# Reading the moving operand of 48 projection units in a woven token order, and dividing the matmuls of four units at token 192

## The chip, the cores and the metric

The kernel runs on one core of one Trainium2 chip. The metric is the device time of one execution in microseconds, lower being better. Before the change it is 1238.59 us (median of two runs, 1238.34 and 1238.84).

## The reference

One inference step of a one-layer decoder: a Mamba-2 SSD branch and a causal pooling branch, each gated per channel, summed and projected. There are 336 tokens: 16 meta tokens, 256 prompt tokens and 64 sample tokens (8 sequences of 8). After the first stages only the last 320 count. Width is 2048. Cut to what matters here:

```python
proj = xn @ w_in                       # 2048 -> 13344 columns
z_ssd, xbc, dt_raw, z_pool, u, gate_ssd, gate_pool = split(proj)
...                                    # conv, SSD recurrence, gated group norm: y
branch_ssd = y @ w_proj_ssd            # 2048 x 2048
mixed = einsum(pooled(u), pool_mix_w) + pool_mix_b      # four groups of 512 x 512
p_out = mixed * pool_scale * silu(z_pool)
branch_pool = p_out @ w_proj_pool      # 2048 x 2048
merged = sigmoid(gate_ssd) * branch_ssd + sigmoid(gate_pool) * branch_pool
h_new = h + merged @ w_out             # 2048 x 2048, then an RMS norm
```

## The kernel before

Everything is kept transposed: channels on the 128 partitions, tokens along the free axis. The weight matrices are cut into **units**, each of which makes 128 output channels for all tokens from 2048 input channels. A unit is 16 k-tiles of 128 x 128 weights, loaded in two halves of 512 KB. The list `UNITS` (`_units()`) fixes the order by hand: `B`, `C`, `xs` and `z` first, with the SSD stages woven between them, then `gs` (gate of the SSD branch, 16 units) alternating with `br` (`w_proj_ssd`), then `u`, `zp` (the pooling branch's z, 16 units) and `mix`, then `gp` (gate of the pooling branch, 16 units, the last zp and mix among the first of them), then `bp` (`w_proj_pool`, 16 units) and `wo` (`w_out`, 16 units).

Precision is kept by splitting each float32 operand into a rounded part `hi` and a rest `lo`, both of type float32r. For each k-tile `half_k` issues three matmuls into the same PSUM tile `acc`: `hi` weights times the high part of the data (L212), `hi` weights times the low part (L213), `lo` weights times the high part (L214). Their moving operands are `xh`/`xl` for projections of the input, `yh`/`yl` for `br`, `ph`/`pl` for `bp` and `mh`/`ml` for `wo`. A unit is thus 48 matmuls. From `gs` on the moving operand is 128 x 320 in most units, read token after token from SBUF (a projection of the input starts at token 16, `NMETA`).

Weights arrive on SP's DMA queue (`raw`). ScalarE rounds each half to `hi` (L144), and VectorE subtracts to get `lo` (L150), about three halves ahead of their use, from rings of four buffers. `acc` is a ring of three PSUM tiles. A unit is evacuated right after it, while the next one runs: `gs_evac` (L760), `zp_evac` (L736) and `gp_evac` (L773) are one ScalarE activation each, 128 x 320 from PSUM to SBUF, and `bp_evac` (L781) multiplies by the gate on VectorE. The program's order on each engine is the order in which this code issues it (`manual_schedule`); `at`, `later` and `tick` put an evacuation and its followers a quarter of a unit or more behind.

Matmuls outside the units matter for reading the profile: the sum over tokens at the end (L817, a 128 x 128 float32 stationary operand and a moving operand of one column), the sum of squares over channels for the group norm (L672, float32, 320 columns), and some in the SSD stages. A float32 matmul is shown by the trace as two MATMUL rows, a float32r matmul as one.

## Time and profile before

| | before |
|---|---|
| median of the runs | 1238.59 us |
| span of the profiled execution | 1239.1 us |
| PE busy, weight loads busy | 1203.4 us, 1165.4 us |
| DVE, ACT, POOL busy | 728.4, 557.7, 159.4 us |
| MATMUL rows, LDWEIGHTS rows | 8066, 8066 |
| first gs evacuated, last | 413.7 us, 602.8 us |
| first zp evacuated, last | 696.1 us, 879.6 us |
| first gp evacuated, last | 888.0 us, 998.8 us |
| matmuls of bp | 997.9 to 1110.5 us |

Engines: PE is TensorE's matmuls and PEld its weight loads, which have rows of their own; DVE is VectorE, ACT ScalarE, POOL GpSimd, SP the queue of DMA issues. Matmul rows overlap: a row lasts from its first token until its result is written, and the next one starts long before that. So the distance from one start to the next (called pitch below) tells what a matmul costs in a full stream, and the duration of a row does not. The profiled execution's span is 0.5 us above the median of the runs.

### The profile page before, as it was taken

The numbers are of one execution on the slowest core, as the hardware profiler recorded it, in microseconds if no ns is written. First come the engines' busy times: TensorE is split into PE (matmuls) and PEld (weight loads), VectorE is DVE, ScalarE is ACT, GpSimd is POOL, SyncE is SP. The second block draws the span as 40 slices with busy tenths as digits, with TensorE's granted clock in tenths as the row PEclk, the third lists the DMA queues.
The fourth block names the chain that finished last, engine by engine and source line by source line (L and its number), as shares of the span: only waits on it lengthen the run. The fifth ranks groups of instructions, "written<-read, shape, count | busy, mean of one in ns | idle before, by whom it ended". The sixth has DMA issues, their size and how long they took to land.

```text
span 1239.1 us, 19826 instructions
## 1 busy us (share of the span) xinstructions
PE 1203.4 (97%) x8066; PEld 1165.4 (94%) x8066; DVE 728.4 (59%) x1008; ACT 557.7 (45%) x792; POOL 159.4 (13%) x161
## 2 busy tenths in 40 slices
PE   6999999999999999999999999999999999999995
PEld 4988988888988999999999999999999999999995
DVE  8798789888887733433445465564343345554543
ACT  4356575748474633333334443434343333334441
POOL 7251142425344000000000000000000000000000
PEclk9999999999999999999999999999999999999998
DMA  5335637475746444444456545554444444456432
GB/s 221 125 125 182 219 126 257 146 243 170 246 143 212 152 156 151 154 153 144 150 161 174 161 150 164 156 156 153 154 153 150 144 149 154 152 170 208 151 120 85
DMA packets 82715, 202.49 MB, mean 163 GB/s; under 512 B 26512, under 2 KB 31280, under 8 KB 82608
## 3 DMA queue, kind: packets, MB, share of 16 engines
q1 hardware_dynamic: 82256, 199.58, 49.9%
q0 software_dynamic: 368, 1.65, 0.4%
q8 instruction: 63, 1.03, 0.3%
q14 instruction: 28, 0.23, 0.1%
HBM read 186.34 MB, written 15.32 MB: 163 GB/s over the span
## 4 chain that ended last, share of the span: by engine, by line
PE 83%; DVE 7%; issue 5%; POOL 3%; ACT 1%; DMA 1%; DVEq 0%; SPq 0%; POOLq 0%; ACTq 0%
PE acc L212 27%; PE acc L213 26%; PE acc L214 26%; DVE lo L150 2%; POOL hin L624 2%; DVE cacc L320 1%; DVE wl L230 1%; DVE x L282 1%; DMA raw<-wall 1%; PE ps_st L565 1%; PE ps_y L579 1%; POOL ss L667 1%; DVE hn L955 0%; POOL bm L482 0%; DVE hin L632 0%
## 5 line engine op out<-in xcount | busy, mean ns | idle before, releaser
L150 DVE TENSOR_TENSOR lo<-raw,hi 128x1024 fp32r<-128x1024 f32 x312 | 392.6, 1260 | 352.6 <-ACT hi L144 352.5
L144 ACT ACTIVATE hi<-raw 128x1024 fp32r<-128x1024 f32 x312 | 329.8, 1058 | 530.5 <-PE acc L213 438.3
L212 PE MATMUL acc<-xh,hi 128*128 128x320 f32 (+4 forms) x1536 | 480.5, 313 | 0.0
L213 PE MATMUL acc<-xl,hi 128*128 128x320 f32 (+4 forms) x1536 | 477.9, 311 | 0.0
L214 PE MATMUL acc<-xh,lo 128*128 128x320 f32 (+4 forms) x1536 | 476.9, 310 | 0.7 <-DVE lo L150 0.7
L212 PEld LDWEIGHTS acc<-xh,hi 128*128 128x128 f32 x1536 | 288.8, 188 | 2.6 <-issue 1.3
L214 PEld LDWEIGHTS acc<-xh,lo 128*128 128x128 f32 x1536 | 288.9, 188 | 1.0 <-DVE lo L150 1.0
L213 PEld LDWEIGHTS acc<-xl,hi 128*128 128x128 f32 x1536 | 288.7, 188 | 1.2
L213 PE MATMUL acc<-pl,hi 128*128 128x320 f32 x256 | 79.4, 310 | 0.0
L214 PE MATMUL acc<-ph,lo 128*128 128x320 f32 x256 | 79.3, 310 | 0.0
L212 PE MATMUL acc<-mh,hi 128*128 128x320 f32 x256 | 79.2, 309 | 0.0
L213 PE MATMUL acc<-ml,hi 128*128 128x320 f32 x256 | 79.1, 309 | 0.0
L214 PE MATMUL acc<-mh,lo 128*128 128x320 f32 x256 | 79.1, 309 | 0.0
L212 PE MATMUL acc<-ph,hi 128*128 128x320 f32 x256 | 79.1, 309 | 0.0
L212 PE MATMUL acc<-yh,hi 128*128 128x320 f32 x256 | 78.7, 308 | 0.0
L213 PE MATMUL acc<-yl,hi 128*128 128x320 f32 x256 | 78.7, 308 | 0.0
L214 PE MATMUL acc<-yh,lo 128*128 128x320 f32 x256 | 78.7, 308 | 0.0
L624 POOL TENSOR_TENSOR hin<-hin,E 128x512 f32<-128x512 f32 x32 | 50.9, 1618 | 52.4 <-ACT E L542 41.9
L320 DVE SCALAR_TENSOR_TENSOR cacc<-rawf,par,cacc 128x360 f32<-128x360 f32 (+1 forms) x72 | 49.1, 682 | 2.1 <-ACT cacc L316 0.4
L212 PEld LDWEIGHTS acc<-ph,hi 128*128 128x128 f32 x256 | 48.4, 189 | 0.0
L213 PE MATMUL acc<-wl,hi 128*128 128x336 f32 (+1 forms) x128 | 43.7, 341 | 4.8 <-DVE wl L230 4.7
L214 PEld LDWEIGHTS acc<-ph,lo 128*128 128x128 f32 x256 | 48.2, 188 | 0.0
(221 smaller groups left out, 1436.8 us busy)
## 6 DMA issues: line engine op xcount, KB each, us to landing
raw<-wall SPq DMA_DIRECT2D x312, 512.0 KB, 3.5
hin<-ssmT SPq DMA_DIRECT2D x16, 512.0 KB, 6.8
ossms<-hin SPq DMA_DIRECT2D x16, 512.0 KB, 5.8
bc<-acT SPq DMA_DIRECT2D x8, 672.0 KB, 6.9
hn<-xT SPq DMA_DIRECT2D x4, 640.0 KB, 6.9
x<-xT SPq DMA_DIRECT2D x3, 672.0 KB, 8.2
opool<-u SPq DMA_DIRECT2D x16, 100.0 KB, 3.1
oconv<-rawf SPq DMA_DIRECT2D x24, 45.5 KB, 4.0
```

What stands on the lines that cost most here:

```text
L144: S.activation(hi, r, AF.Copy)
L150: V.tensor_tensor(out=lo, in0=r, in1=hi.bitcast(F32), op=ALU.subtract)
L212: PE.matmul(acc[:, :n], lhsT=hi[:, c], rhs=bh, start=first, stop=False)
L213: PE.matmul(acc[:, :n], lhsT=hi[:, c], rhs=bl, start=False, stop=False)
L214: PE.matmul(acc[:, :n], lhsT=lo[:, c], rhs=bh, start=False, stop=last)
L230: V.scalar_tensor_tensor(out=wl[q][:, c, :], in0=xg[q][:, c, :], scalar=pc("norm_w", k), in1=wh[q][:, c, :].bitcast(F32), op0=ALU.mult, op ...
L282: V.scalar_tensor_tensor(out=x, in0=x, scalar=pc("norm_w", k), in1=rstd, op0=ALU.mult, op1=ALU.mult)
L320: V.scalar_tensor_tensor(out=a[:, a0:], in0=r[:, a0 + k:k + ACCW], scalar=pc("conv_w", 4 * c + k), in1=a[:, a0:], op0=ALU.mult, op1=ALU.add)
L565: PE.matmul(p, lhsT=st["bt"][:, i, :], rhs=st["xdt"][:, i, :], start=(i == 0), stop=False)
L579: PE.matmul(p[64 * e:64 * e + 64, a:b], lhsT=st["xdt"][:n, i, 64 * hh:64 * hh + 64], rhs=m[:n, e, o:o + b - a], start=(i == 0), stop=(i == ...
L624: GP.tensor_tensor(out=hv, in0=hv, in1=E, op=ALU.mult)
L667: later(1, lambda: GP.tensor_tensor(out=gn[g], in0=gn[g], in1=sq, op=ALU.add))
```

## The change

`WEAVE` names a run length for three kinds of unit: 2 for `gs`, 4 for `zp`, 16 for `gp`. Their moving operand's 320 tokens are seen as two halves of 160, and each matmul reads a run of that many tokens from the first half, then as many from the second, then the next run of the first, and so on. With runs of two the order is 0, 1, 160, 161, 2, 3, 162, 163 and so on. The read from SBUF thus has three dimensions. The output view has the same shape but its columns lie in a row in PSUM, so the result stands there in woven order, written without a jump. The three evacuations read PSUM in the order that undoes it (`unwoven`) and write the old layout. Each of the three kinds has 16 units, that is 768 matmuls.

For `bp` units 12 to 15, `half_k` issues each of the 48 matmuls twice, over tokens 0 to 191 and 192 to 319, with the same weights. Some comment lines are dropped as well. Nothing else differs, and the weights, loads and evacuations of other units stand where they stood.

```diff
@@ -63,6 +63,7 @@
 UNITS = _units()
+WEAVE = {"gs": 2, "zp": 4, "gp": 16}
...
@@ -206,9 +207,28 @@
-    def half_k(acc, w, kk, bh, bl, n, first, last):
+    def woven(a, r, c):
+        return a.rearrange("p (r j c) -> p j r c", r=r, c=c)
+
+    def unwoven(a, r, c):
+        return a.rearrange("p (j r c) -> p r j c", r=r, c=c)
+
+    def half_k(acc, w, kk, bh, bl, n, first, last, weave=0, cut=False):
         hi, lo = w
         c = slice(128 * kk, 128 * kk + 128)
+        if cut:
+            for h, l, f, e in ((hi, bh, first, False), (hi, bl, False, False), (lo, bh, False, last)):
+                for j in range(2):
+                    t = (slice(0, 192), slice(192, n))[j]
+                    PE.matmul(acc[:, t], lhsT=h[:, c], rhs=l[:, t], start=f and j == 0, stop=e, skip_group_check=True)
+            return
+        if weave:
+            bh, bl = woven(bh, 2, weave), woven(bl, 2, weave)
+            o = acc[:, :n].rearrange("p (j r c) -> p j r c", r=2, c=weave)
+            PE.matmul(o, lhsT=hi[:, c], rhs=bh, start=first, stop=False)
+            PE.matmul(o, lhsT=hi[:, c], rhs=bl, start=False, stop=False)
+            PE.matmul(o, lhsT=lo[:, c], rhs=bh, start=False, stop=last)
+            return
         PE.matmul(acc[:, :n], lhsT=hi[:, c], rhs=bh, start=first, stop=False)
...
@@ zp_evac
-        S.activation(pool["z", g][:, c, :], acc[:, 0:TV], AF.Silu)
+        w = WEAVE["zp"]
+        S.activation(pool["z", g][:, c, :].rearrange("p (r j c) -> p r j c", r=2, c=w), unwoven(acc[:, 0:TV], 2, w), AF.Silu)
@@ gs_evac
-        S.activation(t, acc[:, 0:TV], AF.Sigmoid)
+        w = WEAVE["gs"]
+        S.activation(t.rearrange("p (r j c) -> p r j c", r=2, c=w), unwoven(acc[:, 0:TV], 2, w), AF.Sigmoid)
@@ gp_evac
-        S.activation(gpv[q][:, c, :], acc[:, 0:TV], AF.Sigmoid)
+        w = WEAVE["gp"]
+        S.activation(gpv[q][:, c, :].rearrange("p (r j c) -> p r j c", r=2, c=w), unwoven(acc[:, 0:TV], 2, w), AF.Sigmoid)
@@ quarter_mm
-            half_k(acc, w, kk, bh, bl, n, k == 0, k == 15)
+            half_k(acc, w, kk, bh, bl, n, k == 0, k == 15, WEAVE.get(kind, 0), kind == "bp" and idx >= 12)
```

On PE, at the start of `bp` unit 12, the rows were these before (`ph` and `pl` are the high and low part of the moving operand, `hi` and `lo` of the weights; numbers are buffers):

```order
L212 MATMUL acc_10613<-ph_7139,hi_0_10516 128x320
L213 MATMUL acc_10613<-pl_7140,hi_0_10516 128x320
L214 MATMUL acc_10613<-ph_7139,lo_0_10531 128x320
L212 MATMUL acc_10613<-ph_7139,hi_0_10516 128x320
L213 MATMUL acc_10613<-pl_7140,hi_0_10516 128x320
```

In the changed kernel the same place, where L223 is the matmul of the `cut` branch, reads:

```order
L223 MATMUL acc_10613<-ph_7139,hi_0_10516 128x192
L223 MATMUL acc_10613<-ph_7139,hi_0_10516 128x128
L223 MATMUL acc_10613<-pl_7140,hi_0_10516 128x192
L223 MATMUL acc_10613<-pl_7140,hi_0_10516 128x128
L223 MATMUL acc_10613<-ph_7139,lo_0_10531 128x192
L223 MATMUL acc_10613<-ph_7139,lo_0_10531 128x128
```

Each matmul has become two, with the same operands. PE has 7858 rows in this list instead of 7666, 192 more; the other engines have as many as before. The woven matmuls stand where the plain ones stood, as L228, L229 and L230, 768 of each, with the same sizes.

## The prediction

> **What bounds the kernel now.** I read the page's head first, then the clock, then the chain, then the stretches of time in which the touched units lie.

> ```profile
> PE 1203.4 (97%) x8066; PEld 1165.4 (94%) x8066; DVE 728.4 (59%) x1008; ACT 557.7 (45%) x792; POOL 159.4 (13%) x161
> PEclk9999999999999999999999999999999999999998
> PE acc L212 27%; PE acc L213 26%; PE acc L214 26%; DVE lo L150 2%; POOL hin L624 2%; DVE cacc L320 1%; DVE wl L230 1%; DVE x L282 1%; DMA raw<-wall 1%; PE ps_st L565 1%; PE ps_y L579 1%; POOL ss L667 1%; DVE hn L955 0%; POOL bm L482 0%; DVE hin L632 0%
> ```

> PE is busy 97% of the span, its clock is granted nearly in full all along, and the chain that ended last is for 79% the three matmuls of `half_k`. Since matmul rows overlap, busy time alone proves little, so the question is whether PE ever stands still where the change lies. The gs units start soon after 400 us and the cut ones end near 1111 us. The view by stretches of time has, for each engine, busy us and rows:

> ```profile
> 400.00:500.00 100.00, 100.00 (x682) 99.84 (x681) 48.35 (x47) 42.62 (x48) 2.98 (x2) 1.00 0.47 153
> 700.00:800.00 100.00, 100.00 (x674) 100.00 (x674) 54.47 (x74) 43.40 (x66) 0.00 (x0) 1.00 0.51 156
> 1000.00:1100.00 100.00, 100.00 (x681) 100.00 (x680) 53.55 (x71) 36.33 (x42) 0.00 (x0) 1.00 0.46 148
> sum 800.00, PE 800.00 PEld 799.84 DVE 380.82 ACT 315.16 POOL 2.98; mean PE 100.00 PEld 99.98 DVE 47.60 ACT 39.40 POOL 0.37
> ```

> The sum is over eight such stretches, 400 to 1200 us. PE never idles there, the clock is 1.00, VectorE is busy 48% and ScalarE 39%, and the DMA engines about half. Everything that the change touches lies in that stretch. So a nanosecond more or less per touched matmul goes into the end one for one, and nothing another engine does there counts until it exceeds PE's pace by a factor of two.

> What sets PE's pace is to be seen just ahead of the first cut unit, in order of time (start, duration):

> ```profile
> 1081.96 0.31 PE L214 MATMUL acc<-ph,lo 128*128 128x320 f32 x1
> 1081.96 0.19 PEld L212 LDWEIGHTS acc<-ph,hi 128*128 128x128 f32 x1
> 1082.11 0.31 PE L212 MATMUL acc<-ph,hi 128*128 128x320 f32 x1
> 1082.11 0.19 PEld L213 LDWEIGHTS acc<-pl,hi 128*128 128x128 f32 x1
> 1082.26 0.31 PE L213 MATMUL acc<-pl,hi 128*128 128x320 f32 x1
> 1082.26 0.19 PEld L214 LDWEIGHTS acc<-ph,lo 128*128 128x128 f32 x1
> ```

> Each matmul starts together with the weight load of the next. L212 and L213 use the same weights one after the other, and still each has a load of its own: equal weights are not kept. The pitch over all bp units comes from the row of L213 (every third matmul, first and last start):

> ```profile
> L213 PE MATMUL acc<-pl,hi x256: 307/309/317, 997.9 to 1110.5; 128*128 128x320 f32 x128
> ```

> (1110.5 - 997.9) / 255 / 3 = 147.2 ns per matmul of 320 tokens.

> **The cut, costed.** It turns 4 units x 48 = 192 matmuls into 384 with 192 and 128 tokens, and as every matmul loads its weights, it adds 192 loads. How fast matmuls can follow when they are short is shown at the end of the program, where the sum over tokens uses 128 x 128 weights for a moving operand of one column:

> ```profile
> 1225.37 0.83 PE L817 MATMUL ps_fin<-ones,fsq 128*128 128x1 f32 x6 [1.08 <-ACT fsq L801]
> 1225.37 0.74 PEld L817 LDWEIGHTS ps_fin<-ones,fsq 128*128 128x128 f32 x6 [1.34 <-ACT fsq L801]
> L817 PEld LDWEIGHTS ps_fin<-ones,fsq x6: 186/192/192, 1225.4 to 1225.9; 128*128 128x128 f32 x6
> L817 PE MATMUL ps_fin<-ones,fsq x6: 250/250/271, 1225.4 to 1226.0; 128*128 128x1 f32 x6
> ```

> Six rows in a row take 0.83 us, the last one 0.25 of it: (0.83 - 0.25) / 5 = 116 ns. The six loads give (0.74 - 0.19) / 5 = 110 ns. There is next to nothing to stream, so some 112 ns is what one load of 128 columns takes before the next can begin. A load there lasts 192 ns, as the loads of float32r weights above do (0.19 us), and I take the same floor for these. Streaming alone is shorter. The group norm's float32 matmul, two rows of 320 tokens each, gives the scale:

> ```profile
> 344.24 0.70 PE L672 MATMUL ps_gn<-ss,ones 128*128 128x320 f32 x2
> L672 PE MATMUL ps_gn<-ss,ones x8: 432/432/537, 303.7 to 415.0; 128*128 128x320 f32 x8
> ```

> 0.70 less the last row's 0.43 is 270 ns from one start to the next. A float32r matmul of as many tokens has a pitch of 147.2, little over half. If it streams at twice the pace, as I estimate, its stream is 135 ns (0.42 ns a token) and some 12 ns are a surplus that it pays each time. Then 192 tokens take 81 + 12 = 93 ns and 128 take 54 + 12 = 66 ns, both under 112. So both halves are bound by the load: 2 x 112 - 147.2 = 76.8 ns more per old matmul, 192 x 76.8 ns = **14.7 us**. Bounds: if the loads hid completely, only the surplus is paid twice, 192 x 12.2 ns = 2.3 us; if the surplus comes on top of the load floor, 2 x 124 - 147.2 = 101 ns, 19.4 us. I take 14.7, the value whose floor was measured with 128-column loads. It lies on PE alone; the longer units give VectorE and ScalarE more time, not less.

> [...]

> **The weave, costed.** It adds no instruction. 2304 matmuls (768 per kind) read their moving operand in runs of 2, 4 or 16 tokens of four bytes. No matmul of this trace reads with a jump, so its price has to be bounded. From below: nothing, or even a gain of the whole surplus of 12 ns, should that come from how the stream is read. From above: the stream at half pace, which is the 270 ns row, 123 ns more per matmul. The nearest rows are other engines' reads in short runs. ScalarE evacuates 272 tokens in one run and 64 tokens in eight runs of eight:

> ```profile
> L309 ACT ACTIVATE rawf<-acc 128x272 f32<-128x272 f32 x16 | 6.0, 376 | 0.0
> L310 ACT ACTIVATE rawf<-acc 128x64 f32<-128x64 f32 x16 | 3.5, 219 | 0.0
> ```

> 208 tokens fewer cost 157 ns less, 0.755 ns a token; then 64 tokens are 48 ns and 171 ns are fixed, as for the long run (376 - 205). Runs of eight cost nothing there. Runs of 16 (gp) are longer than that, runs of 4 (zp) half, and runs of 2 (gs) a quarter. I take nothing for all three, with gs the least certain.

> [...]

> The evacuations read PSUM in the same short runs:

> ```profile
> L760 ACT ACTIVATE gs<-acc x16: 415/417/438, 413.7 to 602.8; 128x320 f32<-128x320 f32 x16
> L773 ACT ACTIVATE gp<-acc x16: 417/418/437, 888.0 to 998.8; 128x320 f32<-128x320 f32 x16
> L736 ACT ACTIVATE zp<-acc x16: 417/418/437, 696.1 to 879.6; 128x320 f32<-128x320 f32 x16
> ```

> If their tokens took twice as long, each would grow by 320 x 0.755 = 242 ns, 48 of them 11.6 us. ScalarE idles 61% of the stretch, the next thing behind them on its queue is the rounding of weights three halves ahead, and `acc` has two more buffers, so nothing of it shows. Without that cover it would cost the 11.6 us.

> **Sum.** Against the profiled execution: 1239.1 + 14.7 + 0 = 1253.8 us. Its span is 0.5 above the median of the runs shown, so for the median I say **1253.3 us**, 1.2% more. A measurement tells about 2% (24.8 us) from no change, so this counts as within.

> **Rivals.**

> *Runs of two collide with the weight loads* (gs dearer by a little). For it: the surplus of 12 ns exists in float32r rows, while a float32 pass at half pace is not known to have it, as if loads took turns with a stream at full pace; shorter runs might double the turns. Against: nothing shows where the surplus arises. Price 768 x 12.2 ns = 9.4 us, time 1262.7.

> *Runs of two are read at half pace* (the slower side). [...] For it: the moving operand is streamed twice as fast here as in the float32 rows, so a slack that hides jumps elsewhere may be gone. Against: the eight-token runs on ScalarE are free. Price 768 x 123 ns = 94 us, time 1347; if each run costs one token's time only (160 x 0.42 = 67 ns), 52 us and 1305. It decides from 13 ns per gs matmul on, where with the cut it passes 24.8 us.

> *A float32r matmul under some width runs at float32's pace.* For it: no float32r row has fewer than 320 tokens, so nothing shows that the pace holds for 192 or 128. Against: nothing in the rows points to a width at which the pace would change. Two rows of 270 ns would then stand for the two halves' tokens: 540 - 147.2 = 393 ns each, 192 times, 75 us, time 1314.

> *The load floor does not bind float32r* (the cut nearly for nothing): 1238.6 + 2.3 = 1240.9. For it: the floor was read from float32 matmuls. Against: the load rows have the same length. [...]

> *The weave takes the surplus away*: 2304 x 12.2 = 28.1 us less, with the cut 1225.2. For it only that the surplus is unexplained.

> That the change does nothing at all is excluded: the matmuls stand in the program as 384 instead of 192, and no load was shared in the rows above.

> **How the numbers follow.** Chances: forecast 0.59, collision 0.13, free cut 0.09, half pace 0.10, slow narrow matmuls 0.06, a gain 0.03. The first three make 0.81 and lie between 1240.9 and 1262.7, and the load floor's upper bound gives 1258; with some room for a dearer collision the range is 1240 to 1270. Slower by over 2% (over 1263.4): half pace and slow narrow matmuls, 0.16, and half of the collision, which ends at that line: 0.23 in all. Faster by over 2% needs the gain and the free cut together: 0.01. Within: 0.76.

> **What would show it.** In the profile after, the cut rows of 192 and 128 tokens should both have a pitch near 112 ns, and bp units 12 to 15 should take 43 us instead of 28. Pitches near 93 and 66 mean that loads hide; near 324 and 216, that narrow matmuls are slow. The pitch of gs, zp and gp should stay at 146 to 148 ns: if gs shows about 159, it is the collision, 210 to 270 the half pace, and 135 the gain. The three evacuations may grow, with PE still never idle from 400 to 1220 us. The forecast is wrong if gs is off by more than 13 ns per matmul or the cut by more than 5 us.

## The result, and the profile after

The changed kernel takes 1309.91 us (1309.73 to 1310.10) against 1238.59: a ratio of 1.0569, 95% interval 1.0543 to 1.0594. It is 71.3 us slower. The forecast was 1253.3 us within 1240 to 1270, so it was wrong.

The head of the page after, and the chain that ended last:

```profile
span 1308.0 us, 20210 instructions
PE 1270.9 (97%) x8258; PEld 1226.5 (94%) x8258; DVE 728.4 (56%) x1008; ACT 558.1 (43%) x792; POOL 159.9 (12%) x161
PE acc L233 15%; PE acc L232 15%; PE acc L234 15%; PE acc L228 10%; PE acc L229 10%; PE acc L230 10%; PE acc L223 3%; DVE lo L151 2%; POOL hin L644 2%; DVE cacc L340 1%; DVE wl L250 1%; DVE x L302 1%; DMA raw<-wall 1%; POOL bm L502 1%; POOL ss L687 1%
```

PE has 192 more matmuls and 67.5 us more busy time; VectorE, ScalarE and GpSimd stand where they stood. By stretches of time (busy us and rows of each engine, then clock and DMA):

```profile
400.00:500.00 100.00, 100.00 (x545) 96.13 (x544) 41.47 (x40) 35.53 (x40) 2.96 (x2) 1.00 0.35 121
700.00:800.00 100.00, 100.00 (x669) 100.00 (x668) 56.66 (x81) 43.03 (x68) 0.00 (x0) 1.00 0.52 157
1100.00:1200.00 100.00, 100.00 (x774) 100.00 (x774) 44.46 (x58) 32.01 (x38) 0.00 (x0) 1.00 0.44 153
```

PE never idles from 400 to 1200 us, as before, and the clock there is still 1.00, but the stretch that holds gs has 545 matmuls in 100 us where it had 682. Nothing waits; the matmuls themselves are longer. A gs unit of the kernel before, in order of time (start, duration):

```profile
484.77 0.31 PE L212 MATMUL acc<-xh,hi 128*128 128x320 f32 x1
484.91 0.31 PE L213 MATMUL acc<-xl,hi 128*128 128x320 f32 x1
485.06 0.31 PE L214 MATMUL acc<-xh,lo 128*128 128x320 f32 x1
```

Each of these rows lasts 0.31 us and the next starts 0.14 to 0.15 us after it. Ahead of bp unit 12 VectorE waits for the last row of unit 11 and reads `acc` 0.04 us after the end of that row (1082.40 + 0.31):

```profile
1082.40 0.31 PE L214 MATMUL acc<-ph,lo 128*128 128x320 f32 x1
1082.75 0.49 DVE L781 TENSOR_TENSOR bpt<-acc,gp 128x320 f32<-128x320 f32 x1 [1.32 <-PE acc L214]
```

One gs unit, one zp unit and one gp unit of the changed kernel:

```profile
485.08 0.38 PE L228 MATMUL acc<-xh,hi 128*128 128x320 f32 x1
485.29 0.38 PE L229 MATMUL acc<-xl,hi 128*128 128x320 f32 x1
485.49 0.38 PE L230 MATMUL acc<-xh,lo 128*128 128x320 f32 x1
...
735.00 0.32 PE L230 MATMUL acc<-xh,lo 128*128 128x320 f32 x1
735.16 0.32 PE L228 MATMUL acc<-xh,hi 128*128 128x320 f32 x1
735.31 0.32 PE L229 MATMUL acc<-xl,hi 128*128 128x320 f32 x1
...
940.10 0.32 PE L229 MATMUL acc<-xl,hi 128*128 128x320 f32 x1
940.25 0.31 PE L230 MATMUL acc<-xh,lo 128*128 128x320 f32 x1
940.40 0.32 PE L228 MATMUL acc<-xh,hi 128*128 128x320 f32 x1
```

The starts lie some 0.21 us apart in gs and 0.15 in zp and gp, where all had 0.146 before. From the first to the last start of a unit (47 steps) the pitch is 207.5 ns in gs (about 206 in its first four units), 153.3 in zp (153.9 in its last four units) and 151.6 in gp; before it was 146.6, 146.1 to 146.6 and 146.1. The cut units:

```profile
L223 PEld LDWEIGHTS acc<-pl,hi x128: 190/192/192, 1136.9 to 1179.2; 128*128 128x128 f32 x128
L223 PE MATMUL acc<-pl,hi x128: 245/275/304, 1136.9 to 1179.3; 128*128 128x192 f32 x64, 128*128 128x128 f32 x64
```

From 1136.8 to 1179.5 us, first start to last, there are 384 matmuls: 111.6 ns each, where 192 had 147.2. The two halves do not have that pitch each: in the trace a matmul of 192 tokens is followed after 140 ns on average and one of 128 after 83, 223 for the pair, while the weight loads start every 112 ns without a change. The loss by its places, with gs taken at 207.5 throughout:

| part | per matmul | count | us |
|---|---|---|---|
| gs, runs of 2 | 207.5 - 146.6 = 60.9 ns | 768 | 46.8 |
| zp, runs of 4 | 7.2 ns (mean of four groups) | 768 | 5.5 |
| gp, runs of 16 | 151.6 - 146.1 = 5.5 ns | 768 | 4.2 |
| cut | 2 x 111.6 - 147.2 = 76.0 ns | 192 | 14.6 |
| sum | | | 71.1 |

That is the measured 71.3. The profiled span grew by 68.9 only: in the profiled executions gs starts at 402.1 us, where it started at 404.2 before.

### The profile page after: what moved, and what is told of

Same layout as the page of the kernel before. It is cut to its first block, busy times and chain, and to the rows that moved or that the text cites. A ratio compares the mean times of both kernels' runs of the same rounds, so it can differ in the third digit from the quotient of the medians.

```text
span 1308.0 us, 20210 instructions
## 1 busy us (share of the span) xinstructions
PE 1270.9 (97%) x8258; PEld 1226.5 (94%) x8258; DVE 728.4 (56%) x1008; ACT 558.1 (43%) x792; POOL 159.9 (12%) x161
## 4 chain that ended last, share of the span: by engine, by line
PE 80%; issue 7%; DVE 7%; POOL 3%; ACT 1%; DMA 1%; SPq 0%; DVEq 0%; POOLq 0%; ACTq 0%
PE acc L233 15%; PE acc L232 15%; PE acc L234 15%; PE acc L228 10%; PE acc L229 10%; PE acc L230 10%; PE acc L223 3%; DVE lo L151 2%; POOL hin L644 2%; DVE cacc L340 1%; DVE wl L250 1%; DVE x L302 1%; DMA raw<-wall 1%; POOL bm L502 1%; POOL ss L687 1%
## 5 line engine op out<-in xcount | busy, mean ns | idle before, releaser
L228 PE MATMUL acc<-xh,hi 128*128 128x320 f32 x768 | 260.0, 339 | 0.0
L229 PE MATMUL acc<-xl,hi 128*128 128x320 f32 x768 | 259.7, 338 | 0.0
L230 PE MATMUL acc<-xh,lo 128*128 128x320 f32 x768 | 259.6, 338 | 0.0
L232 PE MATMUL acc<-xh,hi 128*128 128x336 f32 (+4 forms) x768 | 244.1, 318 | 0.0
L234 PE MATMUL acc<-xh,lo 128*128 128x336 f32 (+4 forms) x768 | 240.0, 313 | 0.7 <-DVE lo L151 0.7
L233 PE MATMUL acc<-xl,hi 128*128 128x336 f32 (+4 forms) x768 | 240.1, 313 | 0.0
L230 PEld LDWEIGHTS acc<-xh,lo 128*128 128x128 f32 x768 | 147.2, 192 | 3.1
L229 PEld LDWEIGHTS acc<-xl,hi 128*128 128x128 f32 x768 | 146.8, 191 | 2.9
L228 PEld LDWEIGHTS acc<-xh,hi 128*128 128x128 f32 x768 | 146.8, 191 | 2.9
L232 PEld LDWEIGHTS acc<-xh,hi 128*128 128x128 f32 x768 | 144.4, 188 | 2.0 <-issue 0.5
L234 PEld LDWEIGHTS acc<-xh,lo 128*128 128x128 f32 x768 | 144.4, 188 | 1.0 <-DVE lo L151 1.0
L233 PE MATMUL acc<-pl,hi 128*128 128x320 f32 x192 | 59.5, 310 | 0.0
L234 PE MATMUL acc<-ph,lo 128*128 128x320 f32 x192 | 59.4, 309 | 0.0
```

What stands on the lines that cost most here:

```text
L228: PE.matmul(o, lhsT=hi[:, c], rhs=bh, start=first, stop=False)
L229: PE.matmul(o, lhsT=hi[:, c], rhs=bl, start=False, stop=False)
L230: PE.matmul(o, lhsT=lo[:, c], rhs=bh, start=False, stop=last)
L232: PE.matmul(acc[:, :n], lhsT=hi[:, c], rhs=bh, start=first, stop=False)
L233: PE.matmul(acc[:, :n], lhsT=hi[:, c], rhs=bl, start=False, stop=False)
L234: PE.matmul(acc[:, :n], lhsT=lo[:, c], rhs=bh, start=False, stop=last)
```

## The experiments

In what follows (r, c) means: the row of 320 tokens is seen as r pieces, and the read takes c tokens of each piece in turn. The change's gs is (2,2). Four tokens, 16 bytes of a partition, are called a line, after the step from runs of two (207.5 ns) to runs of four (153.3); that it matters where a line begins is shown by the shifts of the second scan. Pitches are taken as above, from the starts of a unit's 48 matmuls. The edits are shown shortened, and what stands behind # in them is a remark. The scans keep the cut and put their orders in place of the change's weave, each scan in one run; their plain br and wo units show 146.6 to 147.0 ns, where the kernel before has 146.7, so pitches can be compared from scan to scan.

**The parts alone.** First the cut without a weave, and the weave of gs without the rest.

```diff
-WEAVE = {"gs": 2, "zp": 4, "gp": 16}
+WEAVE = {}                 # cut alone: plain reads and evacuations
...
+WEAVE = {"gs": 2}          # gs alone: zp, gp plain, and no cut
```

> The cut of bp units 12 to 15 alone, no weave. If the load floor is all that the cut costs: 384 pitches of 112 ns, 14.6 us more than before, 1253.2 us. If the cut and the weave also hinder each other in the changed kernel (a rival), another number than the 14.6 us that its cut units show: under 1248 or over 1258.

Measured: 1254.55 us, ratio 1.0123 (1.0107 to 1.0139), 15.9 us more than the 1238.62 of the kernel before, measured beside it; the interval, 13.3 to 17.2 us, holds the 14.6. Its bp units 12 to 15 show 112 ns, those ahead of them 147.2.

> The weave of gs with runs of two alone, no cut, zp and gp plain. If the price stands in the gs matmuls alone: 768 x 60.9 ns = 46.8 us, 1285.4 us, with a pitch of 207.5 in gs and the old one in zp and gp (146.1). If zp and gp suffer from something gs leaves behind, more than 1288.

Measured: 1285.89 us, ratio 1.0379 (1.0359 to 1.0398), 47.3 us more; pitch 207.5 in gs, 146.1 in gp. So the cut and the weave of gs each cost by themselves what their own matmuls show, and nothing is handed on to other units. The weaves of zp and gp were not run alone; their 9.7 us are read from their pitches.

**First scan of read orders.** Four units per setting, all in one program.

```diff
-            bh, bl = woven(bh, 2, weave), woven(bl, 2, weave)
-            o = acc[:, :n].rearrange("p (j r c) -> p j r c", r=2, c=weave)
+            bh, bl = woven(bh, r, c), woven(bl, r, c)
+            o = acc[:, :n].rearrange("p (j r c) -> p j r c", r=r, c=c)
+            # last two gp groups: plain order of the read, the output view jumps instead
```

> Twelve groups of four units with other read orders; the outputs are the reference's. Written (r, c): r pieces of the row are visited in turn, c tokens each time. Pitch per matmul in ns. Line theory (a visit to a 16-byte line has a price of about 1.3 ns when it brings two tokens or fewer, and four tokens in one visit go at the stream's pace): gs (2,1) 320 visits, 415 or more; (160,1), every second token, 160 visits of two tokens, 207; (80,1), every fourth token, 320 visits, 415; (80,2), first halves of all lines and then second halves, 207; zp (40,4), every second line, 153; (2,8), (2,32), (2,80) 147 to 153; gp (8,2) and (40,2), pieces 160 and 32 bytes apart, 207. Jump theory (the price is for jumping between far places, 640 bytes apart in gs): (80,2), (160,1), (80,1) near 147, (40,2) near 147, (8,2) in between, (2,1) 268. Write theory (the output view with three dimensions or the order of the write makes the price): the last two gp groups read in plain order and write PSUM in jumps, (2,2) and (2,16), and would show 207 and 152; by the other two theories 147, unless jumps in PSUM have a price of their own.

Measured, in ns: (2,1) **135.8**; (160,1) 284.8; (80,1) 289.4; (80,2) 284.8; (40,4) 146.1; (2,8) 150.5; (2,32) 148.3; (2,80) 147.3; (8,2) 310.0; (40,2) 290.0; plain read with jumping writes (2,2) 146.1 and (2,16) 146.1. Rows of (2,1), then of (80,2), then of the plain read whose write jumps:

```profile
405.05 0.30 PE L252 MATMUL acc<-xh,lo 128*128 128x320 f32 x1
405.19 0.30 PE L250 MATMUL acc<-xh,hi 128*128 128x320 f32 x1
405.32 0.30 PE L251 MATMUL acc<-xl,hi 128*128 128x320 f32 x1
...
610.10 0.46 PE L252 MATMUL acc<-xh,lo 128*128 128x320 f32 x1
610.38 0.46 PE L250 MATMUL acc<-xh,hi 128*128 128x320 f32 x1
610.67 0.46 PE L251 MATMUL acc<-xl,hi 128*128 128x320 f32 x1
...
1079.89 0.31 PE L250 MATMUL acc<-xh,hi 128*128 128x320 f32 x1
1080.04 0.31 PE L251 MATMUL acc<-xl,hi 128*128 128x320 f32 x1
1080.19 0.31 PE L252 MATMUL acc<-xh,lo 128*128 128x320 f32 x1
```

The steps are 0.135, 0.285 and 0.15 us. The write theory fell: the jumps of these two patterns in the output cost nothing. The jump theory fell: (2,1) jumps most of all and is faster than plain order, and (80,2), which never goes farther than the next line, is among the slowest. The line theory as it stood fell too. By it (2,1) and (80,1) come to another line 320 times and should both take 415; one takes 135.8, the other 289.4, hardly more than the 284.8 of (80,2), which makes 160 visits and was to take 207.

**Second scan: shifts, half the weights, float32.**

```diff
+            h, l = h[:, 0:64], l[:, 0:64]                                # half the weight columns
+            h, l, bh, bl = (x.bitcast(F32) for x in (h, l, bh, bl))      # float32 in place of float32r
...
-            bh, bl = a[k // 4][:, k % 4, lo:T], b[k // 4][:, k % 4, lo:T]
+            bh, bl = a[k // 4][:, k % 4, lo - s:T - s], b[k // 4][:, k % 4, lo - s:T - s]
```

> Twelve more groups of four units. Some read tokens shifted by one or two places (the gates then belong to neighbouring tokens, so the output differs), some use 64 of the 128 weight columns (half the channels stand twice), and 12 units use the float32 type instead of float32r. Line theory: gs (2,4) shifted by two tokens, each run lies in two lines, 207; shifted by one, also two lines, 207; plain order shifted by two or by one 147 to 148; zp (2,2) shifted by one, three visits for four tokens, up to 311. Jump theory: (2,4) shifted stays at 153, (2,2) shifted at 207. If the surplus of 12 to 13 ns over the stream comes from weight loads taking turns with the stream: 64 columns in plain order 140, (2,4) 143; if not, 147 and 153. (2,2) with 64 columns: 207 if loads have no part in it, under 190 if they do. Float32 at half pace: plain 270; with runs of two 270 if a visit has a price in time that the slower stream hides (line theory), 331 or more if each run adds a delay of its own; runs of one: 270 to 415.

Measured: (2,4) shifted by two tokens 208.3, by one 208.2, against 153.3 unshifted; so a run of four tokens is dear where it lies in two lines of 16 bytes, as each now does. Plain order shifted by two 147.7, by one 144.4. (2,2) shifted by one 206.1, not 311. With 64 weight columns plain order takes 144.9, (2,4) 153.3, (2,2) 207.1: a load of half as many columns, whose row lasts 136 ns instead of 188, takes off less than 2 ns, so weight loads have next to no part in any of it, neither in the surplus nor in the price. Float32, for each of a matmul's two rows: plain 269, (2,2) 280, (2,1) 339. Rows of float32 (two rows a matmul, shown as one entry) with (2,2), then with (2,1):

```profile
1040.62 0.72 PE L250 MATMUL acc<-xh,hi 128*128 128x320 f32 x2
1041.18 0.72 PE L251 MATMUL acc<-xl,hi 128*128 128x320 f32 x2
...
1149.95 0.84 PE L252 MATMUL acc<-xh,lo 128*128 128x320 f32 x2
1150.63 0.84 PE L250 MATMUL acc<-xh,hi 128*128 128x320 f32 x2
```

**Third scan, chosen for what only one of the two theories allows.** Blocks of 2d tokens, read 0, d, 1, d+1 and so on.

```diff
+            bh, bl = (x.rearrange("p (j r c) -> p j c r", r=2, c=d) for x in (bh, bl))
+            o = acc[:, :n].rearrange("p (j c r) -> p j c r", r=2, c=d)
```

> Twelve groups of four units, two of them shifted by one or two tokens (the output differs there), one with 64 weight columns (half the channels stand twice). Blocks of 2d tokens read as 0, d, 1, d+1 and so on, that is pairs d tokens apart: gs d = 16, 4, 8, 2, zp group 3 shifted. Two-stream theory, pitch in ns: d = 4, 8 and 16: 136, as each stream takes four tokens of a line in a row; d = 2: each stream takes two tokens of a line in a row, as plain order does, 146. Place theory (what helps is that neighbours in the order come from two far places): all four stay at 146 or go up. zp: four pieces by one token, tokens 0, 80, 160, 240, 1: each stream changes line at each token, 206 by the two-stream theory; place theory 136. (2,1) with 64 columns 134 to 136; (2,1) shifted by one and by two tokens 136 and 136. Float32 has one stream by this theory, pitch of one of the two rows: every second token (160,1) 270 to 285, two tokens of a line in a row; first and second halves of lines (80,2) 270 to 285; every fourth token (80,1) one of a line, 340 or more; pairs four apart 340 or more. If the type makes no difference to the rule, (160,1) and (80,2) are over 500.

Measured: d = 4, 8 and 16 all 135.8; d = 2 146.6; (2,1) with 64 columns 135.8, shifted by one or two 136.1; four pieces by one token **170.5**. Float32 per row: (160,1) 282, (80,2) 282, (80,1) 564, pairs four apart 340. Rows of d = 4, of d = 2, and of float32 for (160,1) and for (80,1):

```profile
452.07 0.30 PE L254 MATMUL acc<-xl,hi 128*128 128x320 f32 x1
452.20 0.30 PE L255 MATMUL acc<-xh,lo 128*128 128x320 f32 x1
452.34 0.30 PE L253 MATMUL acc<-xh,hi 128*128 128x320 f32 x1
...
546.02 0.31 PE L255 MATMUL acc<-xh,lo 128*128 128x320 f32 x1
546.17 0.31 PE L253 MATMUL acc<-xh,hi 128*128 128x320 f32 x1
546.32 0.31 PE L254 MATMUL acc<-xl,hi 128*128 128x320 f32 x1
...
869.84 0.72 PE L254 MATMUL acc<-xl,hi 128*128 128x320 f32 x2
870.40 0.72 PE L255 MATMUL acc<-xh,lo 128*128 128x320 f32 x2
...
984.47 1.29 PE L253 MATMUL acc<-xh,hi 128*128 128x320 f32 x2
985.58 1.30 PE L254 MATMUL acc<-xl,hi 128*128 128x320 f32 x2
```

Pairs four tokens apart, neighbouring lines, do as well as pairs 160 apart, so distance is not what helps; pairs two apart do no better than plain order. In float32 the steps from matmul to matmul are 0.56 us with two tokens of a line and 1.11 to 1.13 with one, which is the factor of two. The place theory falls. One number was missed: four pieces by one token was to take 206 and took 170.5. By the theory each stream there changes its line at every token but takes turns between two lines only and comes back to each three more times. Halved, the float32 rows show the same for a stream of that kind, and the orders, but for runs of whole lines (see the last scan), fall into one scale, with the theory's streams:

| tokens a stream takes from a line in a row | float32r, ns | float32, half of a row, ns |
|---|---|---|
| four | 135.8 | 134.6 |
| two | 146.1 to 146.6 | 140 to 141 |
| one, comes back three times, each time after one other line | 170.5 | 170 |
| one, comes back once, after one or two other lines: (2,2) and the shifted (2,4) | 206 to 208 | not run |
| one, comes back only after seven or more other lines | 285 to 310 | 282 |

The sizes of the rows with "comes back" were read off and not foretold. What lies behind these sizes was not seen.

**The change with runs of one.**

```diff
-WEAVE = {"gs": 2, "zp": 4, "gp": 16}
+WEAVE = {"gs": 1, "zp": 1, "gp": 1}
```

> The change with runs of one token in all three kinds, cut kept: tokens 0, 160, 1, 161 and so on. Two-stream theory, formed after the scans: a float32r matmul takes the tokens at even and at odd places of its order as two streams, and each stream wants at least two tokens in a row from the same 16-byte line. With runs of one each stream runs through one half in plain order, so 2304 matmuls have the pitch of 135.8 that the first scan shows, 10.6 ns less than before: 24.4 us less, with the cut 14.6 more, 1228.8 us. Jump theory (each jump has a price): runs of one jump most, over 1310.

Measured: 1230.4 us, ratio 0.9922 (0.9905 to 0.9940); the kernel before, beside it, 1239.64. The same weave with runs of one makes the kernel 9 us faster in spite of the cut; the woven units show 135.8.

**Runs of one wherever 320 tokens are read, no cut.** On the kernel before, with `two` and `back` as views that undo the order in each evacuation:

```diff
+        if n == TV:
+            bh, bl = (x.rearrange("p (r j) -> p j r", r=2) for x in (bh, bl))
+            o = o.rearrange("p (j r) -> p j r", r=2)
...
-        S.activation(t, acc[:, 0:TV], AF.Sigmoid)
+        S.activation(two(t), back(acc), AF.Sigmoid)
```

> No cut. All units with 320 tokens (116 of 156, 5568 matmuls) read tokens 0, 160, 1, 161 and so on, and their evacuations read PSUM back in plain order. Two-stream theory: pitch 135.8 in place of 146.1 to 147.2, 5568 x 10.6 ns = 59 us less, 1180 us; in the z stage PE waits a few per cent of the time, so up to 8 us of that may stay away, 1188. If the gain needs something of the gates alone (their operand, their place), under 30 us less.

Measured: 1186.67 us, ratio 0.9576 (0.9561 to 0.9591), 53 us less than the 1239.64 beside it, 4.2%. It beats both kernels. By stretches of time:

```profile
400.00:500.00 100.00, 100.00 (x736) 99.84 (x735) 51.79 (x51) 45.34 (x50) 1.49 (x1) 1.00 0.51 168
600.00:700.00 100.00, 100.00 (x704) 100.00 (x703) 53.54 (x72) 42.82 (x65) 0.00 (x0) 1.00 0.56 170
1000.00:1100.00 100.00, 100.00 (x738) 100.00 (x737) 55.64 (x71) 41.66 (x51) 0.00 (x0) 1.00 0.54 187
```

738 matmuls in 100 us where there were 681, PE without idle time as before, and 135.8 ns in every unit from gs to wo but the u units, which stand as they were (704 rows). The gain of 53 is 6 short of 59, within what the expectation left for the z stage, and the trace shows it missing there: from the first z matmul to the first of gs it has 155.7 us where the trace before has 157.4, 1.7 us less instead of 8.

**What runs of whole lines still cost.** The same code as in the first scan with other (r, c).

> What runs of whole lines still cost (zp 7 ns, gp 5.5 ns per matmul in the changed kernel). Outputs are the reference's. Pitch over the 146.1 to 146.6 of plain order. Back theory: the price is for going back to an earlier place, once a round over all pieces; with 0.2 ns or so each time, (2,4) goes back 40 times for 7 ns, so (4,4) 20 times 3 to 4 ns, (8,4) 10 times 2, (10,4) 8 times 1.5, (20,4) 4 times 1; (4,16), (10,16), (4,40) under 1.5. Distance theory: the price is for each jump, forward or back, to a place farther than the next lines, and falls with the distance: (4,4) and (8,4) 7 as (2,4) has, (20,4), 64 bytes apart, near 0; (4,16) 5, (4,8) 4. Float32 with runs of 16 and of 4, whole lines at half pace: 269 to 271 if the slower stream hides the price, 275 or more if not.

Measured: (4,4) 142.2, (8,4) 153.3, (10,4) 154.8, (20,4) about 142, (4,16) 147.3, (10,16) 151.6, (4,8) 145.9, (10,8) 147.8, (2,40) 148.6, (4,40) 146.1; float32 with runs of 16 and of 4, 269. Both theories fall. The price does not go with the number of jumps back, nor does it shrink with their distance, and some orders beat plain order. With runs of four, 640, 160 and 128 bytes between the pieces are dear (153.3, 153.3 and 154.8) and 320 and 64 cheap (142.2 and about 142), with no order that I can name. In float32 the two orders that were run show nothing of it (269, as in plain order). In all of these orders each stream takes two tokens of a line in a row, so the two-stream description does not tell 142 from 155 either. What makes the difference there stays open; it is 9.7 us of the 71.

## Why the prediction was wrong

- *PE is the bound and each nanosecond per touched matmul counts in full*: right. The places' sum, 71.1, is the measured loss, and PE waits for nothing from gs to the end of wo's stream, as before.
- *The cut costs 14.7 us, because a load of 128 columns takes 112 ns*: right, by the floor read from L817. The units show loads every 112 ns, 111.6 ns per matmul and 14.6 us, alone and in the changed kernel. The sign that was named, 112 ns for both widths, did not come: the steps are 140 and 83, and only their sum, 223, is two steps of the loads. The two rivals on the cut, free loads (2.3 us) and float32's pace (75 us), are out.
- *The evacuations' short reads stay hidden*: right, and more, since they cost next to nothing. The medians are 418 ns in gs, 419 in zp and 422 in gp, against 417, 418 and 418 before.
- *The weave costs nothing, "with gs the least certain"*: **this step failed**. The term stood at 0 in the sum and came to 56.5 us: 46.8 in gs, 5.5 in zp and 4.2 in gp, all of it as longer pitches of the woven matmuls. The nearest row that I took was ScalarE's, 0.755 ns a token, while PE takes 0.46 in plain order (146.6 ns for 320 tokens) and 0.42 with runs of one (135.8). That row could not carry the step for two more reasons. By the code, L310 reads its 64 tokens of `acc` in one piece and only writes them in eight runs. And the 0.755 is worked out from the same two rows that are then found to agree, so a price of the runs would have gone into it unseen. No row of the trace before bounds what a read in runs of two costs on PE. The half pace of 270 ns, named as the upper bound, is none either: (8,2) takes 310.
- *Runs of two are read at half pace*: the text itself named the faster stream as a reason for this outcome, and gave it a chance of 0.10. Its lower form, one token's time for each run, 52 us and 1305, came nearest in size (46.8 in gs), by coincidence: runs of one are twice as many and make the matmul 10.8 ns shorter. The half pace itself, 270 ns, is not what gs has, at 207.5. Near it lies (80,2), at 284.8, where a line gives two tokens and is left until all others have given theirs; gs is not that order, since by the two-stream description each stream comes back to its line after one other.
- *Runs of two collide with the weight loads*: out, as half as many weight columns left 207.1.
- *The surplus of 12 ns per matmul* was real. The rival "the weave takes the surplus away" came true, though for runs of one and not for those of the change: 146.6 to 135.8. By the two-stream description it comes of the two tokens of a line that each stream takes in plain order, where four leave next to none (135.8 against 134.6, half of a float32 row).

That the price is one of the read order is shown: with the same number of loads and tokens, and PSUM written in a row, the pitch goes from 10.8 ns below plain order to 164 above. What the runs cannot show is the hardware behind "two streams". It is the description that foretold the d = 2, 4, 8 and 16 orders and the float32 orders before they ran (the 564 only as "340 or more"). It missed 170.5 and says nothing of the 142 to 155 of whole lines.

## What to carry to other kernels

Where PE never idles, as here from 400 to 1200 us, the read order of the moving operand is a cost in itself: 135.8 to 310 ns for the same 320 float32r tokens in these runs. What described it best was to look at float32r orders in pairs: the longer places 0, 2, 4 and places 1, 3, 5 of the order each stayed in a 16-byte line, the shorter the matmul (four tokens in a row 135.8 ns, two 142 to 155, one 170.5 to 310). Interleaving two halves token by token (135.8), or the two halves of each eight tokens (d = 4, also 135.8), does that; the output stands interleaved in PSUM and the evacuation that reads it back in order costs nothing extra (gs 417 ns in the faster kernel as before). A nearest row is worth little as a bound if it comes from an engine that reads more slowly, as ScalarE did here (0.755 ns a token against PE's 0.46): even on PE the same (2,2) costs 11 ns a row in float32, where a plain row takes 269, and 61 in float32r, where it takes 146.6.

## What the hardware showed that I had not expected

- A plain contiguous read is not the fastest float32r read: 146.6 ns for 320 tokens against 135.8 with runs of one.
- Every second token, (160,1), takes 284.8 ns in float32r, though two tokens of each line are used in a row; in float32 it takes 282 instead of 269 a row.
- Jumps in PSUM writes of runs of two or 16 tokens cost nothing (146.1, as in plain order).
- A plain read that starts one token ahead of a line's start is a little faster, 144.4 ns against 146.1 to 146.6, and one that starts two ahead a little slower, 147.7.
